# The far output product of dilated attention in four row-group parts: 32 keys at a time into four PSUM banks

## The chip, the cores and the metric

The kernel runs on one core of one Trainium2 chip. The metric is the device time of one execution in microseconds (us), from the median of several runs; the profile describes one such execution. The engines are TensorE (PE in the profile, with its weight loads shown apart as PEld), VectorE (DVE), ScalarE (ACT), GpSimd (POOL) and SyncE (SP), which only issues transfers here. TensorE multiplies a stationary operand of up to 128 rows (the contraction) by 128 columns, which a LDWEIGHTS puts into the array, with a moving operand that a MATMUL streams through it; the sums land in PSUM, which has eight banks of 512 float32 per partition.

## The reference

Two layers of a causal decoder trunk over 512 tokens of width 1024, in float32. Layer 0 mixes tokens with three groups of dilated sliding-window attention, eight heads of width 128 in each group; layer 1 with a pooling mixer; a SwiGLU FFN follows each. Only the attention of layer 0 touches this change:

```python
ATTN_PAIRS = ((128, 1), (512, 4), (2048, 16))
o = jnp.einsum('bnhqk,bnkhd->bnqhd', p / den, vb)   # per group, dilated by 1, 4, 16
wts = jax.nn.softmax(jnp.stack(lses, axis=0), axis=0)
o = jnp.sum(wts[..., None] * o, axis=0)             # the three groups of a head add up
return o.astype(h.dtype) @ w_out
```

With 512 tokens, group 0 (dilation 1) has four blocks of 128 queries that see their own and the previous block; group 1 (dilation 4) has four residue classes of 128 tokens, each a full 128 by 128 causal product; group 2 (dilation 16) has sixteen classes of 32 tokens, each a product of 32 queries with 32 keys. The kernel scales the probabilities of the three groups by the merge weights first, so that the outputs of a head are plain sums of three products.

## The kernel before

Everything is kept with channels on the 128 partitions and the 512 tokens along the free dimension. Projections are done in pairs by a scheme with seven half products instead of eight (`seven`, `values12`, and `chained` in the FFN); each weight is split in two fp32r parts by ACT (L92) and DVE (L93), and each product is three fp32r passes (L461 to L463, L632 to L634, L329 to L332). Weights stream from HBM through rings of buffers, in an order fixed by the queues `loads` and `steps`, which `pump` advances one step after each piece of a product.

Attention is written between those pieces. For heads 1 to 7 the loop runs `seven` for the query/key pair of each group, then the values; `between(h, g)` names the attention functions of an earlier head that are called after a given piece: for even h, `output(h-2)` after the second piece of g = 0 and `output(h-1)` after the third piece of g = 2. Heads 6 and 7 have their outputs after the loop, each followed by `halve`, which splits the result for the output projection (L1009 to L1018). The engines take their instructions in the order in which the functions are called; a wait is a semaphore that the program sets where one engine needs another's result or a free buffer.

Before `output(h)` come three steps on the same head. `scores0` and `scores12` form the scores (L716 for group 0 in pieces, L736 for group 1, L740 for group 2), `merge` scales the exponentials, and `turn0` and `turn12` transpose them, so that keys lie on the partitions: `own` and `before` hold group 0, `t12[:, 0]` group 1 and `t12[:, 1]` group 2. For group 2 four classes share the 128 partitions: class j takes partitions 32j to 32j+31, as a diagonal block of 32 by 32 in a 128 by 128 matrix that `zero` cleared once.

`output(h)` then multiplies values (stationary) with probabilities (moving), all in float32. The trace shows each float32 product of the program as two hardware passes, so that L847's 64 products stand there as 128 instructions.

- L840 and L841: seven products for group 0 into one PSUM bank, which ACT copies to `o[h]` in another order of the tokens (L843).
- L847: for each of four classes r the product of group 1 and that of group 2, which add up in a second bank. Group 2's product is a full 128 by 128 by 128 one, zeros included.
- L850: DVE adds the second bank to `o[h]`.

PSUM tiles come from one pool of eight banks (`ps`); a new tile takes a bank whose last reader is done.

Of the kernel before, what the change touches and what calls it, by code (L numbers as in the profile page):

```python
# [15 lines left out]
P = 128  # L16
S = 512
# [7 lines left out]
NT = S // P  # L25
NI = P // NT
G = P + NI
Y16 = NT * NT
# [12 lines left out]
WARM = 5  # L41
NOUT = 3
NSOLO = 2
PARTS = ((0, 2, False), (2, 10, True), (10, 18, True), (18, 22, False))
ENDS = 5
BACK = {"blocks": 3, "sums": 7}
# [19 lines left out]
def trunk(ctx: ExitStack, tc: tile.TileContext, xT, xN, norms, w_first, w_qk, w_qkp, w_v0, w_v0p, w_v12, w_out, w_outp, w_pair, w_down, w_dblock, w_pin, w_pgrp,  # L66
          consts, ident_in, invcnt_in, outT, outR):
    nc = tc.nc
# [14 lines left out]
    def ps():  # L83
        return psum.tile([P, S], F32, tag="ps", name="ps")
# [134 lines left out]
    def pairs(*srcs, shift=LINE // 4, back=False):  # L219

        these = [Pair(src, shift, back) for src in srcs]
        for parts in zip(*(p.steps() for p in these)):
            steps.extend(parts)
        units.append((these,))
# [11 lines left out]
    def plain(*srcs, lean=False):  # L236
        for src in srcs:
            share(1, src, lean=lean)

    for h in range(HEADS):  # L240
        if h == 0:
            plain(*[w_qk[u] for u in range(len(QK) - NF)])
        for g in range(3):
            if h == 1 and g < NSOLO:
                plain(*[w_qk[len(QK) - NF + 2 * g + c] for c in range(2)])
            elif h:
                pairs(w_qkp[3 * h - 3 - NSOLO + g])
        if h == 0:
# [10 lines left out]
    def ffn_plan(layer):  # L259
        j = 0  # L260
        for i, (first, end, block) in enumerate(PARTS):
            while j < min(max(end + block, NPLAIN), FC):
# [5 lines left out]
            if block:  # L268
                for m in range(K2):
                    pairs(w_dblock[sum(p[2] for p in PARTS) * layer + sum(p[2] for p in PARTS[:i]), m],  # L270
                          shift=0, back=True)
# [103 lines left out]
    def product(layer):  # L375
        return Product(KC, stream(layer)).add(range(KC)).p
# [27 lines left out]
    def rstd(parts):  # L404

        nt = parts[0].shape[1] // P
        pc = ps()
        for i, a in enumerate(parts):
            for t in range(nt):
                for c in range(0, P, NI):  # L410
                    nc.tensor.matmul(pc[c:c + NI, t:t + 1], a[:, t * P + c:t * P + c + NI], ones,
                                     start=i == t == 0, stop=i == len(parts) - 1 and t == nt - 1)
        v = tmp.tile([P, nt], F32, tag="var", name="var")
        nc.vector.tensor_scalar(v, pc[:, :nt], 1.0 / D, EPS, op0=OP.mult, op1=OP.add)
        r, n = tmp.tile([P, nt], F32, tag="rcol", name="rcol"), nt // 2
        for t in range(0, nt, n):
            nc.gpsimd.tensor_tensor(r[:, t:t + n], v[:, t:t + n], nhalf[:, :n], op=OP.pow)
        return [r[:, t:t + 1] for t in range(nt)]
# [177 lines left out]
    def in_a_row(t):  # L596
        return t.rearrange("p (y x z) -> p x y z", y=Y16, z=2)


    with tc.tile_pool(name="opool", bufs=1) as opool:  # L600
        early = [opool.tile([P, 2, S], F32R, tag=f"o{k}", name="early") for k in range(K2)]
        with tc.tile_pool(name="apool", bufs=1) as apool:
            const = apool.tile([P, 5 * P], F32, name="const")
            d0, d12, swap = const[:, :2 * G], (const[:, 2 * G:2 * G + P], const[:, 2 * G + P:3 * G]), const[:, 3 * G:3 * G + P]
            rows = {}
            QKV = {}
# [86 lines left out]
            def blk(t, b, n=1):  # L693
                return t[:, b * P:(b + n) * P]
# [136 lines left out]
            def output(h):  # L831
                (own, before), t12 = A[h]["t0"], A[h]["t12"]

                def v0(b):
                    return blk(QKV[h // 2, 0, 2][:, b, :], h % 2)

                po = ps()
                for b in range(NT):
                    if b > 0:
                        nc.tensor.matmul(blk(po, b), v0(b - 1), before[:, b - 1], start=True, stop=False)  # L840
                    nc.tensor.matmul(blk(po, b), v0(b), own[:, b], start=b == 0, stop=True)  # L841
                o0 = o[h]
                nc.scalar.copy(in_a_row(o0), po.rearrange("p (x y z) -> p x y z", y=Y16, z=2))  # L843
                po = ps()
                for r in range(NT):
                    for g in (1, 2):
                        nc.tensor.matmul(blk(po, r), blk(QKV[h // 2, 12, 2][:, r, :], h % 2 * 2 + g - 1),  # L847
                                         t12[:, g - 1, r, :],
                                         start=g == 1, stop=g == 2)
                nc.vector.tensor_add(o0, o0, po)  # L850


            late = [apool.tile([P, S], F32R, tag=tag, name="early") for tag in ("t0", "o0")]
# [5 lines left out]
            H, T, o = {}, {}, []  # L859
# [49 lines left out]
            for k in range(KC):  # L909
# [15 lines left out]
                for j, (w, v) in enumerate(((hi, 0), (hi, 1), (lo, 0))):  # L925
                    for i, f in enumerate(lead):
                        c = (k % 2 * NF + i) * P
# [34 lines left out]
            for c in range(2):  # L962
                p = product(0)
# [108 lines left out]
    with tc.tile_pool(name="fpool", bufs=2) as fpool:  # L1072
# [3 lines left out]
        def ftile(name, n=S):  # L1076
            return fpool.tile([P, PAD + S], F32, tag="f", name=name, bufs=6)[:, :n]
# [8 lines left out]
        def ffn(layer, nxt, lead, row):  # L1086
# [324 lines left out]
        r = rstd([t, sq])  # L1411
# [115 lines left out]
```

## Time and profile before

| | before |
|---|---|
| median of 3 runs | 1185.73 us (1185.5 to 1185.83) |
| span of the profiled execution, first to last instruction | 1184.0 us |
| PE busy | 1175.4 us (99%) |
| PEld busy (weight loads, overlapping PE) | 1119.9 us (95%) |
| DVE busy | 989.0 us (84%) |
| ACT busy | 721.7 us (61%) |
| POOL busy | 171.3 us (14%) |
| granted TensorE clock | 0.9 or more of full speed in every slice of the page |

For the profiled execution no time is given beside its span; the median of the runs lies 1.7 us above it. Attention with its projections runs from the start to about 435 us; the eight calls of `output` start at 112, 139, 214, 241, 316, 343, 420 and 430 us.

How to read the rows: a group row gives line, engine, operation, what it writes and reads, rows and columns of the stationary operand (128*32), size of the moving one (128x32), the count, then busy time in us (overlaps counted once), the mean ns of one, the engine's idle time before them and what ended it. A MATMUL's duration includes its way through the array, so consecutive ones overlap; the pace is the distance from start to start. A chain row gives start, length and the work on the path that ended last. A timeline row gives start, length and, in brackets, the engine's idle time before it.

### The profile page before, as it was taken

How to read it: one execution, taken by the hardware profiler on the slowest of the kernel's cores; microseconds unless marked ns; L12 is line 12 of the kernel's file. 1: busy time of each engine (PE TensorE's matmuls, PEld its weight loads, DVE VectorE, ACT ScalarE, POOL GpSimd, SP SyncE). 2: the span in 40 equal slices, each digit the busy share in tenths (PEclk: the TensorE clock that was granted, in tenths of full speed). 3: DMA queues.
4: the chain of work that ended last, by engine and by line, in shares of the span. 5: the costliest groups of instructions: out<-in, count | busy, mean ns of one | idle time of the engine just before them, and what ended most of it. 6: DMA issues, size and time to landing. Idle time of an engine off the chain costs nothing.

```text
span 1184.0 us, 25180 instructions
## 1 busy us (share of the span) xinstructions
PE 1175.4 (99%) x10042; PEld 1119.9 (95%) x10042; DVE 989.0 (84%) x1733; ACT 721.7 (61%) x1262; POOL 171.3 (14%) x165
## 2 busy tenths in 40 slices
PE   9999999999999999999999999999999999999997
PEld 7889999999999989889999999988889999999997
DVE  7997898889789888699988988656789998898875
ACT  6554564546455557747756775775575766676553
POOL 1101111111111002311111111122130111111100
PEclk9999999999999999999999999999999999999999
DMA  8537667666856557957777877798595777877732
GB/s 302 130 95 187 147 153 166 168 160 152 192 140 169 145 157 195 246 113 203 191 188 189 204 184 209 195 265 208 121 195 119 187 199 195 198 191 193 197 92 72
DMA packets 83766, 207.57 MB, mean 175 GB/s; under 512 B 7856, under 2 KB 13120, under 8 KB 83648
## 3 DMA queue, kind: packets, MB, share of 16 engines
q1 hardware_dynamic: 52672, 144.84, 36.9%
q0 software_dynamic: 30688, 60.83, 31.6%
q8 instruction: 78, 1.28, 0.4%
q14 instruction: 40, 0.33, 0.1%
q10 hardware_dynamic: 288, 0.29, 0.1%
HBM read 203.84 MB, written 2.10 MB: 174 GB/s over the span
## 4 chain that ended last, share of the span: by engine, by line
PE 96%; DMA 1%; issue 1%; DVE 1%; ACT 0%; POOL 0%; POOLq 0%; DVEq 0%; ACTq 0%
PE ps L461 21%; PE ps L462 20%; PE ps L463 20%; PE ps L329 7%; PE ps L330 7%; PE ps L332 7%; PE ps L928 2%; PE ps L632 2%; PE ps L633 2%; PE ps L634 2%; DMA raw<-w_outp 1%; PE ps L847 1%; PE ps L716 1%; PE ps L736 1%; PE ps L841 1%
## 5 line engine op out<-in xcount | busy, mean ns | idle before, releaser
L92 ACT ACTIVATE w<-raw 128x1024 fp32r<-128x1024 f32 x268 | 283.7, 1063 | 177.0 <-PE ps L463 73.3
L93 DVE TENSOR_TENSOR w<-raw,w 128x1024 fp32r<-128x1024 f32 x268 | 326.4, 1222 | 48.8 <-ACT w L92 44.7
L461 PE MATMUL ps<-far,w 128*128 128x256 f32 x896 | 246.5, 275 | 0.0
L462 PE MATMUL ps<-far,w 128*128 128x256 f32 x896 | 246.4, 275 | 0.0
L463 PE MATMUL ps<-far,w 128*128 128x256 f32 x896 | 246.4, 275 | 0.0
L461 PE MATMUL ps<-near,w 128*128 128x256 f32 x676 | 190.5, 282 | 0.0
L462 PE MATMUL ps<-near,w 128*128 128x256 f32 x676 | 186.9, 277 | 0.0
L463 PE MATMUL ps<-near,w 128*128 128x256 f32 x676 | 186.9, 276 | 0.0
L462 PEld LDWEIGHTS ps<-far,w 128*128 128x128 f32 x896 | 168.2, 188 | 0.1
L461 PEld LDWEIGHTS ps<-far,w 128*128 128x128 f32 x896 | 168.2, 188 | 0.1
L463 PEld LDWEIGHTS ps<-far,w 128*128 128x128 f32 x896 | 168.2, 188 | 0.0
L461 PEld LDWEIGHTS ps<-near,w 128*128 128x128 f32 x676 | 127.1, 188 | 0.5
L462 PEld LDWEIGHTS ps<-near,w 128*128 128x128 f32 x676 | 127.1, 188 | 0.0
L463 PEld LDWEIGHTS ps<-near,w 128*128 128x128 f32 x676 | 127.0, 188 | 0.0
L329 PE MATMUL ps<-near,w 128*128 128x512 f32 (+1 forms) x316 | 119.4, 379 | 0.0
L332 PE MATMUL ps<-near,w 128*128 128x512 f32 (+1 forms) x316 | 118.7, 376 | 0.0
L330 PE MATMUL ps<-near,w 128*128 128x512 f32 (+1 forms) x316 | 118.7, 376 | 0.0
L173 POOL DMA_DIRECT2D raw<-w_pair x36 | 43.6, 1210 | 291.7 <-DMA raw<-w_pair 87.3
L329 PEld LDWEIGHTS ps<-near,w 128*128 128x128 f32 x316 | 59.3, 188 | 11.0 <-ACT near L92 0.4
L332 PEld LDWEIGHTS ps<-near,w 128*128 128x128 f32 x316 | 59.3, 188 | 10.9
L330 PEld LDWEIGHTS ps<-near,w 128*128 128x128 f32 x316 | 59.4, 188 | 10.6 <-DVE near L93 0.2
L92 ACT ACTIVATE half<-rawhalf 128x512 fp32r<-128x512 f32 x84 | 52.8, 630 | 13.7 <-PE ps L463 11.8
(333 smaller groups left out, 2802.7 us busy)
## 6 DMA issues: line engine op xcount, KB each, us to landing
raw<-w_pair SPq DMA_DIRECT2D x80, 512.0 KB, 4.9
raw<-w_qkp SPq DMA_DIRECT2D x38, 512.0 KB, 4.5
raw<-w_pair POOLq DMA_DIRECT2D x36, 512.0 KB, 7.6
raw<-w_dblock SPq DMA_DIRECT2D x32, 512.0 KB, 4.7
raw<-w_qkp POOLq DMA_DIRECT2D x19, 512.0 KB, 7.5
raw<-w_v SPq DMA_DIRECT2D x18, 512.0 KB, 4.1
rawhalf<-w_pair SPq DMA_DIRECT2D x36, 256.0 KB, 5.2
raw<-w_dblock POOLq DMA_DIRECT2D x16, 512.0 KB, 7.5
```

The costliest lines, as they stand in the source:

```text
L92: nc.scalar.activation(hi, v, AF.Copy)
L93: nc.vector.tensor_tensor(lo, v, hi.bitcast(F32), op=OP.subtract)
L173: nc.gpsimd.dma_start(self.b.rearrange("p (a c) -> p a c", a=2), self.src[:, None, 3 * n:].to_broadcast([P, 2, n]), accum_op=OP.add)
L329: nc.tensor.matmul(self.p[:, cols], w[0][:, s], mh[:, cols], start=self.done == 0, stop=False)
L330: nc.tensor.matmul(self.p[:, cols], w[0][:, s], ml[:, cols], start=False, stop=False)
L332: nc.tensor.matmul(self.p[:, cols], w[1][:, s], mh[:, cols], start=False, stop=self.done == self.n)
L461: nc.tensor.matmul(dst, w.t[0][:, c], th, start=k == 0 and not on, stop=False, skip_group_check=on)
L462: nc.tensor.matmul(dst, w.t[0][:, c], tl, start=False, stop=False, skip_group_check=on)
L463: nc.tensor.matmul(dst, w.t[1][:, c], th, start=False, stop=k == n - 1, skip_group_check=on)
L632: nc.tensor.matmul(o, mh, wh, start=k == 0, stop=False)
L633: nc.tensor.matmul(o, mh, wl, start=False, stop=False)
L634: nc.tensor.matmul(o, ml, wh, start=False, stop=k == K2 - 1)
```

## The change

Only `output` is changed. Group 0's seven products now write straight into the place of their tokens in the final order: the destination is a view of the bank in runs of two neighbouring columns, 32 columns apart. Group 1's four products add to the same bank. Group 2's products are cut along the keys: for each class r four products of 32 keys (rows 32c to 32c+31 of the array), 128 channels and 32 queries, part c into a bank of its own, in 32 columns of it. ACT then copies the shared bank to `o[h]`, and DVE adds the four others, each to a quarter of `o[h]`'s columns. The zeros outside the diagonal blocks are no longer multiplied.

```diff
+ROWS = 4
...
                 po = ps()
+                rows = in_a_row(po)
+
+                def put(dst, v, w, first=False):
+                    nc.tensor.matmul(dst, v, w, start=first, stop=True, skip_group_check=True)
...
                 for b in range(NT):
+                    dst = rows[:, b * NT:(b + 1) * NT]
+                    put(dst, v0(b), own[:, b].rearrange("p (x y z) -> p x y z", y=Y16, z=2), b == 0)
                     if b > 0:
-                        nc.tensor.matmul(blk(po, b), v0(b - 1), before[:, b - 1], start=True, stop=False)
-                    nc.tensor.matmul(blk(po, b), v0(b), own[:, b], start=b == 0, stop=True)
-                o0 = o[h]
-                nc.scalar.copy(in_a_row(o0), po.rearrange("p (x y z) -> p x y z", y=Y16, z=2))
-                po = ps()
+                        put(dst, v0(b - 1), before[:, b - 1].rearrange("p (x y z) -> p x y z", y=Y16, z=2))
                 for r in range(NT):
-                    for g in (1, 2):
-                        nc.tensor.matmul(blk(po, r), blk(QKV[h // 2, 12, 2][:, r, :], h % 2 * 2 + g - 1),
-                                         t12[:, g - 1, r, :],
-                                         start=g == 1, stop=g == 2)
-                nc.vector.tensor_add(o0, o0, po)
+                    put(blk(po, r), v12(r, 1), t12[:, 0, r, :])
+                far = [ps()[:, :S // ROWS].rearrange("p (r q) -> p r q", r=NT) for c in range(ROWS)]
+                n = P // ROWS
+                for r in range(NT):
+                    for c in range(ROWS):
+                        k = slice(c * n, (c + 1) * n)
+                        put(far[c][:, r], v12(r, 2)[k], t12[k, 1, r, k], r == 0)
+                nc.scalar.copy(o[h], po)
+                for c in range(ROWS):
+                    oc = o[h].rearrange("p (r c q) -> p c r q", r=NT, c=ROWS)[:, c]
+                    nc.vector.tensor_add(oc, oc, far[c])
```

`v12(r, g)` is the block of values of class r for group g, as L847 read it.

On PE the stretch of `output(0)`, called from `between(2, 0)`, stands in the program before as follows. L461 to L463 are the projection around it; `t0` holds group 0's probabilities, `t12` the others', `v0` and `v12` the values.

```order
L463 MATMUL ps_1288<-h_658,w_1188 128x256
L841 MATMUL ps_1331<-t0_845,v0_615 128x128
L840 MATMUL ps_1331<-t0_845,v0_615 128x128
L841 MATMUL ps_1331<-t0_845,v0_615 128x128
L840 MATMUL ps_1331<-t0_845,v0_615 128x128
L841 MATMUL ps_1331<-t0_845,v0_615 128x128
L840 MATMUL ps_1331<-t0_845,v0_615 128x128
L841 MATMUL ps_1331<-t0_845,v0_615 128x128
L847 MATMUL ps_1340<-t12_905,v12_1028 128x128 x8
L461 MATMUL ps_1289<-near_82,w_1204 128x256
```

In the changed program the same stretch reads (its lines lie one or more further down; only the first of four rounds of parts is shown, and the other three are the same):

```order
L842 MATMUL ps_1331<-t0_845,v0_615 128x4x16x2 x7
L842 MATMUL ps_1331<-t12_905,v12_1028 128x128 x4
L842 MATMUL ps_1343<-t12_905,v12_1028 128x32
L842 MATMUL ps_1344<-t12_905,v12_1028 128x32
L842 MATMUL ps_1345<-t12_905,v12_1028 128x32
L842 MATMUL ps_1346<-t12_905,v12_1028 128x32
```

Four full products of L847 became sixteen of 32 keys and 32 columns, which go round four banks (ps_1343 to ps_1346), after all full ones; the number of products goes from 15 to 27 per head.

On DVE the end of the same `output` stands so before (L93 and L190 prepare weights, L771 and L774 belong to `merge`):

```order
L93 TENSOR_TENSOR w_1402<-raw_1181,w_1402 128x1024
L850 TENSOR_TENSOR o_1024<-o_1024,ps_1340 128x512
L771 TENSOR_TENSOR far_1229<-ps_1369,place_453 128x64
L774 TENSOR_REDUCE st_935<-far_1229 128x16
```

and so in the changed program:

```order
L94 TENSOR_TENSOR w_1420<-raw_1181,w_1420 128x1024
L863 TENSOR_TENSOR o_1024<-o_1024,ps_1343 128x4x32
L863 TENSOR_TENSOR o_1024<-o_1024,ps_1344 128x4x32
L863 TENSOR_TENSOR o_1024<-o_1024,ps_1345 128x4x32
L863 TENSOR_TENSOR o_1024<-o_1024,ps_1346 128x4x32
L772 TENSOR_TENSOR far_1229<-ps_1387,place_453 128x64
```

One add of 512 columns became four of 128, at the same place in DVE's queue; ACT's copy stays at its place too.

More of the change, by code (lines that the diff above doesn't have):

```diff
@@ L837, in output, with v12 @@
                 po = ps()
+                rows = in_a_row(po)
+                def put(dst, v, w, first=False):
+                    nc.tensor.matmul(dst, v, w, start=first, stop=True, skip_group_check=True)
+                def v12(r, g):
+                    return blk(QKV[h // 2, 12, 2][:, r, :], h % 2 * 2 + g - 1)
                 for b in range(NT):
+                    dst = rows[:, b * NT:(b + 1) * NT]
+                    put(dst, v0(b), own[:, b].rearrange("p (x y z) -> p x y z", y=Y16, z=2), b == 0)
                     if b > 0:
-                        nc.tensor.matmul(blk(po, b), v0(b - 1), before[:, b - 1], start=True, stop=False)
-                    nc.tensor.matmul(blk(po, b), v0(b), own[:, b], start=b == 0, stop=True)
-                o0 = o[h]
-                nc.scalar.copy(in_a_row(o0), po.rearrange("p (x y z) -> p x y z", y=Y16, z=2))
-                po = ps()
-                for r in range(NT):
-                    for g in (1, 2):
-                        nc.tensor.matmul(blk(po, r), blk(QKV[h // 2, 12, 2][:, r, :], h % 2 * 2 + g - 1),
-                                         t12[:, g - 1, r, :],
-                                         start=g == 1, stop=g == 2)
-                nc.vector.tensor_add(o0, o0, po)
+                        put(dst, v0(b - 1), before[:, b - 1].rearrange("p (x y z) -> p x y z", y=Y16, z=2))
+                for r in range(NT):
+                    put(blk(po, r), v12(r, 1), t12[:, 0, r, :])
[9 more added lines that the diff above has]
+                    nc.vector.tensor_add(oc, oc, far[c])
             late = [apool.tile([P, S], F32R, tag=tag, name="early") for tag in ("t0", "o0")]
```

## The prediction

> **What bounds the kernel now.** I read the page first (busy times, chain shares), then the waits, then the chain and the timeline around the eight calls of `output`.
>
> ```profile
> span 1184.0 us, 25180 instructions
> PE 1175.4 (99%) x10042; PEld 1119.9 (95%) x10042; DVE 989.0 (84%) x1733; ACT 721.7 (61%) x1262; POOL 171.3 (14%) x165
> PE 96%; DMA 1%; issue 1%; DVE 1%; ACT 0%; POOL 0%; POOLq 0%; DVEq 0%; ACTq 0%
> ```
>
> TensorE carries 96% of the path and is never idle for long, so whatever `output` adds to or takes from PE's queue moves the end by as much. Busy share does not say whether streaming or weight loading paces PE. The chain shows what one output costs there (start, length, work):
>
> ```profile
> 140.35 1.79 PE ps L847 x16
> 142.14 0.12 PE ps L461
> ...
> 153.04 0.89 PE ps L736 x8
> 153.93 0.39 PE ps L740 x32
> 154.32 0.31 PE ps L461
> 154.63 0.12 PE ps L462
> ```
>
> L847's sixteen passes take 1.79 us, 0.112 each; eight of them are group 2's, so 0.89 us per head is what the change replaces, 7.2 us over eight heads: the most that could ever be saved. Group 0 and group 1 keep their passes. The lower four rows are the nearest thing to the new form: L740 works on a 32-column strip of the array (128*32), four strips side by side.
>
> **What a small tile costs.** Two things are read from L740 and its kin: the pace inside, and what going in and out costs.
>
> ```profile
> 153.86 0.35 PEld L740 LDWEIGHTS ps<-qk,qk 128*32 128x32 f32 x32
> 477.71 0.35 PEld L411 LDWEIGHTS ps<-ones,sq 128*32 128x32 f32 x32 [0.35 <-issue]
> 161.31 0.31 PEld L769 LDWEIGHTS ps<-far,const 128*128 128x128 f32 x2
> L847 PEld LDWEIGHTS ps<-t,v 128*128 128x128 f32 x128 | 14.9, 192 | 0.0
> L740 PEld LDWEIGHTS ps<-qk,qk 128*32 128x32 f32 x256 | 2.8, 112 | 1.0
> L740 PE MATMUL ps<-qk,qk 128*32 128x32 f32 x256 | 3.7, 199 | 0.0
> L411 PE MATMUL ps<-ones,sq 128*32 128x1 f32 x160 | 2.3, 172 | 0.0
> ```
>
> In L740, 32 loads start within 0.35 less one load's 0.112, that is 0.24 us or about 0.0077 each: four strips take a round of four in 0.031 us. L411 streams one column where L740 streams 32, yet its 32 loads take the same 0.35 us. So in these tiles the loads set the pace and not the streaming. A load of 128 columns lasts 192 ns and one of 32 lasts 112: 80 ns for 96 columns, 0.83 ns a column, so 128 columns occupy 0.107 us, all but L847's pace of 0.112. L769 confirms it for the full array: it streams only 64 columns, but its two loads stand 0.31 less 0.19, 0.12 us apart.
>
> The change shortens what is streamed (128 columns to 32) and the contraction (128 rows to 32). It leaves every weight tile 128 columns wide, which is the dimension that a load's time follows in these rows; none of them has fewer than 128 rows. Instead of 8 loads per head there are 32.
>
> The Trainium skill says outright what no run here can show: by TensorE: Matmul & The Clock Gate, section LDWEIGHTS, a load's time goes with its columns alone, and one of 32 rows by 128 columns takes as long as a full one. Its figure for 128 columns, an estimate of 107 ns at 1.2 columns per ns, is what the rows above give (0.107 us). By it the row groups can at best hide the extra loads, not gain; the sum below would be the same.
>
> Going in and out: 32 passes of L740 are eight rounds, 8 x 0.031 = 0.25 us, but take 0.39 in the chain, so 0.14 us is lost on the way in; the next full pass (L461) takes 0.31 instead of 0.12, so 0.19 on the way out. Together 0.33 us each time that the array changes its tiling. `output` has no such change now and gets one per head.
>
> **The sum.** Per head 16 products of 32 keys are 32 passes, four row groups with 8 each.
>
> - If the four row groups run side by side as L740's four strips do, a row group loads 8 x 0.112 = 0.89 us, as long as the 0.89 us removed. The net is the change of tiling, +0.33 us.
> - Bound above: the groups' loads go one after another, 32 x 0.112 = 3.58 us, net 3.58 + 0.33 - 0.89 = +3.02 us per head.
> - Bound below: a load costs by its area and 32x128 passes go at the round of a 128x32 tile, 0.031 us: 0.25 + 0.33 - 0.89 = -0.31 us per head.
>
> I take the first: L740 is nearest in every respect (four tiles, float32, 32 columns streamed), and a round there overlaps four tiles' loads.
>
> Group 0's seven products write the same columns in runs of two; no row has a strided destination. Below, it costs nothing; above, I let each of the 14 passes take twice its 0.112, +1.57 us per head. I take zero: a float32 pass at 0.112 for 128 columns has 0.87 ns for each column to land. The Trainium skill has a rule against it: PSUM — Partial Sum Buffer, section Specifications (TRN2), warns that a non-contiguous pattern slows matmuls significantly, and gives PSUM lines of 8 bytes. The runs here are just 8 bytes long and no run shows such a write; the rule gives no factor, and it is the rival below.
>
> Off PE:
>
> ```profile
> L850 DVE TENSOR_TENSOR o<-o,ps 128x512 f32<-128x512 f32 x8 | 5.5, 685 | 6.1 <-PE ps L847 6.1
> L508 DVE TENSOR_TENSOR sums<-ps,qk 128x256 f32<-128x256 f32 x12 | 4.5, 411 | 0.1
> L843 ACT COPY o<-ps 128x512 f32<-128x512 f32 x8 | 4.9, 607 | 4.3 <-PE ps L841 4.3
> 342.41 0.41 DVE L516 TENSOR_TENSOR qk<-sums,ps 128x256 f32<-128x256 f32 x1
> ```
>
> 256 columns less are 274 ns less, so an add of 128 columns should take 685 - 3 x 137 = 274 ns, four 1.10 us: +0.41 us of DVE per head, 3.3 in all. DVE waits 6.1 us for L847 at its eight adds, so it is early at nearly all of them and this is hidden. Were it not, it would be at most 0.4 us a head. ACT's copy has the same size, but now waits for group 1 as well, some 0.9 us longer, with the next weights' splits queued behind it; PE has no wait for those now (the waits below), and ACT is busy 61%.
>
> Five banks instead of two are taken per output. A far bank may be had when its last reader is through. For odd heads the last reader ahead is L516 of the pair before; the one above ended at 342.82 and `output(5)` reaches L847 at 344.63, so 1.8 us are spare, and the far products start 0.9 us later still. No wait there, and at most some tenths if DVE slips.
>
> The one place where PE waits for other engines lies between the last two outputs:
>
> ```profile
> PE ps L841 <- ACT t L808: 0.8, 1, 0.8
> 408.77 10.49 DMA raw<-w_outp
> 426.53 0.68 DVE L850 TENSOR_TENSOR o<-o,ps 128x512 f32<-128x512 f32 x1
> 427.73 0.62 ACT L92 ACTIVATE near<-o 128x512 fp32r<-128x512 f32 x1
> 429.57 0.49 PE L841 MATMUL ps<-t,v 128*128 128x128 f32 x2 [0.81 <-ACT t L808]
> ```
>
> `output(7)` starts 0.81 us late, behind a chain of transfer, DVE and ACT that begins before `output(6)` at 420. What output 6 adds on PE is swallowed there, so seven heads count, not eight. The first six count in full: the transfer waits for buffers that PE's progress frees, so it moves with them. DVE's extra 0.41 us at 426.53 ends L850 at 427.62 instead of 427.21, just ahead of the ACT split at 427.73 that needs it; uncovered it would cost up to 0.4 us once.
>
> Sum: 7 x 0.33 = +2.3 us. The profiled span of 1184.0 becomes 1186.3; with the 1.7 us that lie between span and median, **1188.0 us**.
>
> **The rivals.**
>
> - Row groups share more than L740's strips do. Two at a time make 16 rounds: 1.79 + 0.33 - 0.89 = +1.23 us per head, less the 0.8 swallowed once: +9.0, 1194.8 us. One at a time: 8 x 3.02 - 0.8 = +23.4, 1209.1 us. For it: no row shows two row groups at once. Against it: strips overlap freely. Chance 16%.
> - The strided destination halves group 0's pace: 8 x 1.57 + 2.3 = +14.9, less what is left of the swallowed 0.8, 0.5: 1200.1 us. For it: nothing in these rows excludes it. Against: 8 bytes in one piece. Chance 12%.
> - The other side, a gain: loads of 32 rows are cheaper than those of 128. At the round of 0.031 us each of seven heads gains 0.31 us, 1183.6 us, and it decides from a round below 0.070 us (8 x 0.070 + 0.33 = 0.89). For it: no row has a load with fewer rows. Against: 0.83 ns a column in each load seen. TensorEngine Tiling (Array Packing) of the Trainium skill, section Theoretical Speedup, promises up to four times for a contraction of 32; its Key Properties name the drain at a change of mode, with which L740's 0.33 us agrees. Taken at full value, and without the drain, 0.89 becomes 0.22 and seven heads gain 4.7 us: 1181.0 us. Chance together 8%.
> - The rest, 2%, is waits for PSUM banks of a few us.
>
> **How the numbers follow.** The forecast has 62%. Its own range is 1186.7 (entry or exit cheaper by half) to 1189.5 (0.2 us more per head). Two tenths of a per cent, about what a measurement of this kernel tells from no change, are 2.4 us; the forecast of +2.3 lies at that line. Of its 62 points I give 29 to slower and 33 to the same. The two rivals above it are slower, 28; of the gain's 8 points I give 5 to faster and 3 to the same, since its 1183.6 is just within the line, and the rest falls 1 to slower, 1 to faster. That makes faster 6%, same 36%, slower 58%. The range 1185.0 to 1200.5 holds the forecast, two groups at a time and the strided case, and leaves out the gain (8%) and one group at a time (8%).
>
> **What would show it.** In the changed profile the 32-row loads of one output should span about 0.9 us with rounds of four some 0.112 us apart; rounds of 0.031 mean the gain, loads each 0.112 after the last mean the serial rival. The full pass after them should take about 0.3 us in the chain instead of 0.12. Group 0's 14 passes should keep 0.112 us each. The four DVE adds should take about 0.27 us each, and the wait list should name only L841's counterpart on ACT, longer or shorter by some tenths. The prediction is wrong if PE waits for DVE or ACT at the far products, or if seven outputs lengthen by other than 0.33 us each.

## The result and the profile after

| | before | changed |
|---|---|---|
| median of 18 runs each, on the same chips | 1186.2 us (1185.29 to 1187.23) | 1188.04 us (1187.74 to 1188.93) |
| span of the profiled execution | 1184.0 us | 1186.8 us |
| DVE busy | 989.0 us | 990.6 us |
| PE instructions | 10042 | 10234 |

The changed kernel takes 1.0016 times as long, with a 95% interval of 1.0010 to 1.0022: 1.2 to 2.6 us slower. Page of the changed kernel, its first rows and the shares of the chain by engine:

```profile
span 1186.8 us, 25595 instructions
PE 1179.2 (99%) x10234; PEld 1122.4 (95%) x10234; DVE 990.6 (83%) x1757; ACT 721.4 (61%) x1262; POOL 170.5 (14%) x165
PE 99%; issue 1%; DVE 0%; POOL 0%; DVEq 0%; POOLq 0%
```

The path now is PE alone. Before, DVE and DMA had 1% each of it; the reason is the short stretch between the last two outputs, told below. The chain around the second output (start, length, work; the change moves line numbers, so that L842 holds all of `output`'s products, and L461 became L462):

```profile
139.81 3.48 PE ps L842 x54
143.29 0.32 PE ps L462
143.61 0.13 PE ps L463
```

and the timeline of its weight loads, and then the groups of L842, of the four adds and of ACT's copy:

```profile
142.20 0.98 PEld L842 LDWEIGHTS ps<-t,v 32*128 32x128 f32 x32
```

```profile
L842 PEld LDWEIGHTS ps<-t,v 128*128 128x128 f32 x176 | 20.4, 192 | 0.5 <-ACT t L809 0.5
L842 PEld LDWEIGHTS ps<-t,v 32*128 32x128 f32 x256 | 7.9, 186 | 1.0
L863 DVE TENSOR_TENSOR o<-o,ps 128x128 f32<-128x128 f32 x32 | 7.0, 282 | 6.9 <-PE ps L842 6.7
L860 ACT COPY o<-ps 128x512 f32<-128x512 f32 x8 | 4.7, 581 | 8.0 <-PE ps L842 8.0
```

The 32 loads of one head start within 0.98 less one load's 0.19, that is 0.79 us. In single records a round is four loads 6.7 ns apart, and the rounds start 0.108 to 0.112 us after one another (142.197, 142.305, 142.414, 142.526 us and so on). So the four row groups do run side by side, but a load of 32 rows lasts 186 ns where one of 128 rows lasts 192, and each round takes as long as one full pass. The Trainium skill's page TensorE: Matmul & The Clock Gate has this rule in its section LDWEIGHTS (a load's time goes with its columns); the two rows above agree with it.

From the start of the last full pass to the start of the second full pass behind, one head takes 1.450 us, where before its eight full passes of the third group and the next one took 1.125: +0.325. Group 0's 14 passes, now with a strided destination, still stand 0.112 us apart. The changed kernel's only wait of PE for another engine:

```profile
PE ps L921 <- DVE idle L918: 1.2, 1, 1.2
```

It was there before, at L908, in the first 5 us of the program; the prediction had called the last output the one place where PE waits. PE waits for no PSUM bank and for nothing at the far products. The wait of 0.8 us of the last output for ACT is gone, while the prediction expected it to be the only one on the list.

Where the time came from is seen by matching PE's passes outside `output` one by one (there are 9802 in both traces). The difference of their start times, changed less before, in us:

| output | last pass ahead of it | second pass behind it | step over the output | step up to the next output |
|---|---|---|---|---|
| 0 | +0.73 | +1.05 | +0.32 | -0.03 |
| 1 | +1.02 | +1.35 | +0.33 | +0.18 |
| 2 | +1.53 | +1.85 | +0.32 | -0.03 |
| 3 | +1.82 | +2.15 | +0.33 | +0.18 |
| 4 | +2.33 | +2.65 | +0.32 | -0.03 |
| 5 | +2.62 | +2.95 | +0.33 | +0.18 |
| 6 | +3.13 | +3.41 | +0.28 | 0.00 |
| 7 | +3.41 | +2.74 | -0.67 | +0.09 to the end |

The first 0.73 arises in the first 15 us, before any changed instruction, and stays constant up to the first output. In the other kernels below it lies anywhere from -0.02 to +0.74, so it belongs to the execution and not to the edit. Without it the profile says +2.1 us, the medians +1.84: seven outputs +2.23, the stretches between them +0.45, the last output -0.67, the end +0.09.

**The stretches between.** Timeline of PE behind output 1, before and then changed; each fence shows the first and the last of a run of equal passes:

```profile
142.33 0.28 PE L461 MATMUL ps<-near,w 128*128 128x256 f32 x1
...
143.58 0.28 PE L463 MATMUL ps<-near,w 128*128 128x256 f32 x1
```

```profile
144.04 0.28 PE L462 MATMUL ps<-tx,w 128*128 128x256 f32 x1
...
145.10 0.28 PE L462 MATMUL ps<-near,w 128*128 128x256 f32 x1
```

Before, 11 passes lie between these two, 1.25 / 11 = 0.114 us each; changed, 9 passes, 1.06 / 9 = 0.118. Over the whole stretch of 96 passes the means are 113.4 and 117.8 ns, at a granted clock of 1.00 in both: 96 x 4.4 ns = 0.42 us. Before had such a slower stretch too, the 60 passes behind the scores (L740) that follow: 117.8 ns there before, 113.6 in the changed kernel, which gives back 0.24 us. So +0.18 after every odd output.

**The last output.** Chain of the kernel before, ahead of its last output, then the timeline of the changed one at the same place:

```profile
424.91 0.32 DVE t L809
...
425.25 0.43 DVE room L1029
...
426.19 0.43 DVE room L1030
...
426.71 0.63 ACT oh L92
427.34 0.12 ACT t L806
```

```profile
427.18 1.24 DVE L810 STREAM_TRANSPOSE t<-s 32x128 f32<-32x128 f32 x4
...
429.45 0.21 ACT L807 COPY t<-ps 32x96 f32<-32x96 f32 x1
...
432.12 0.42 DVE L1043 TENSOR_TENSOR room<-room,o 128x256 f32<-128x256 f32 x1
...
433.16 0.63 ACT L93 ACTIVATE oh<-room 128x512 fp32r<-128x512 f32 x1
```

Before, DVE's second half of `room` (L1030) and ACT's split of it stand between the last transposes and the copies of `turn0` that the last output waits for. The transposes end at 425.23, and the first copy starts at 427.25 on ACT's timeline: 2.0 us. In the changed program the same two instructions (L1043 and the split at 433.16) stand behind those copies, and the way from 428.42 to 429.45 takes 1.0 us. PE came to this place 3.41 us later than before, the last copy that its first product needs ended only 2.64 us later (432.16 against 429.52), and of the 0.81 us of waiting 0.04 are left. Up to the transposes the chain had kept step with PE (3.2 us later); it got ahead behind them. Some of that was lost again, since ACT now waits for the four adds there:

```profile
430.36 0.63 ACT L93 ACTIVATE near<-o 128x512 fp32r<-128x512 f32 x1 [0.33 <-DVE o L863]
```

Another part of the -0.67 is the order of group 0's products. Weight loads before, then PE in the changed kernel:

```profile
430.07 0.30 PEld L840 LDWEIGHTS ps<-t,v 128*128 128x128 f32 x2 [0.20 <-ACT t L806]
```

```profile
432.21 1.54 PE L842 MATMUL ps<-t,v 128*128 128x128 f32 x11
```

Before, the second product (L840, with `before`) waits for the last copy of `turn0` on ACT, which ends at 430.02 us. In the changed kernel a product with `own` stands ahead of it, and PE runs on; by the single records this saves 0.22 us. So the last output adds up: +0.33 for its own change of tiling, -0.77 of waiting, -0.22 by the order of the products.

### The profile page after: what moved, and what is told of

Read it like the earlier page. It is cut to its first block, busy times and chain, and to the rows that moved or that the text cites. A ratio compares the mean times of both kernels' runs of the same rounds, so it can differ in the third digit from the quotient of the medians.

```text
span 1186.8 us, 25595 instructions
## 1 busy us (share of the span) xinstructions
PE 1179.2 (99%) x10234; PEld 1122.4 (95%) x10234; DVE 990.6 (83%) x1757; ACT 721.4 (61%) x1262; POOL 170.5 (14%) x165
## 4 chain that ended last, share of the span: by engine, by line
PE 99%; issue 1%; DVE 0%; POOL 0%; DVEq 0%; POOLq 0%
PE ps L462 21%; PE ps L463 20%; PE ps L464 20%; PE ps L330 8%; PE ps L333 8%; PE ps L331 8%; PE ps L842 2%; PE ps L633 2%; PE ps L635 2%; PE ps L634 2%; PE ps L941 2%; PE ps L717 1%; PE ps L737 1%; PE ps L921 0%; PE ps L425 0%
## 5 line engine op out<-in xcount | busy, mean ns | idle before, releaser
L93 ACT ACTIVATE w<-raw 128x1024 fp32r<-128x1024 f32 x268 | 283.6, 1063 | 176.9 <-PE ps L464 72.9
L462 PE MATMUL ps<-far,w 128*128 128x256 f32 x896 | 246.5, 275 | 0.0
L463 PE MATMUL ps<-far,w 128*128 128x256 f32 x896 | 246.5, 275 | 0.0
L462 PE MATMUL ps<-near,w 128*128 128x256 f32 x676 | 190.8, 282 | 0.0
L463 PE MATMUL ps<-near,w 128*128 128x256 f32 x676 | 187.0, 277 | 0.0
L462 PEld LDWEIGHTS ps<-far,w 128*128 128x128 f32 x896 | 168.2, 188 | 0.1
L463 PEld LDWEIGHTS ps<-far,w 128*128 128x128 f32 x896 | 168.2, 188 | 0.1
L462 PEld LDWEIGHTS ps<-near,w 128*128 128x128 f32 x676 | 127.1, 188 | 0.7
L463 PEld LDWEIGHTS ps<-near,w 128*128 128x128 f32 x676 | 127.1, 188 | 0.0
L93 ACT ACTIVATE half<-rawhalf 128x512 fp32r<-128x512 f32 x84 | 52.8, 630 | 13.9 <-PE ps L464 11.8
```

What stands on the lines that cost most here:

```text
L93: nc.scalar.activation(hi, v, AF.Copy)
L462: nc.tensor.matmul(dst, w.t[0][:, c], th, start=k == 0 and not on, stop=False, skip_group_check=on)
L463: nc.tensor.matmul(dst, w.t[0][:, c], tl, start=False, stop=False, skip_group_check=on)
```

## The experiments

The theory: a round of row groups takes what a load of its columns takes (0.112 us for 128), and changing the tiling costs about 0.33 us per head. Rivals: it is the strided or shared bank, the extra DVE adds, or work off PE that costs the 1.8 us. Each diff is against the changed kernel. Medians are of 4 to 11 runs, and each ratio is against the kernel before on the same chip (medians 1186.51, 1186.07 and 1186.3 us in the three sets). "Section" is the time from the last full pass ahead of the far products to the second full pass behind them; it is 1.125 us before and 1.450 in the changed kernel.

### rows_alone: the parts on row groups, the rest as before

```diff
-                    dst = rows[:, b * NT:(b + 1) * NT]
-                    put(dst, v0(b), own[:, b].rearrange(...), b == 0)
...
+                    nc.tensor.matmul(blk(po, b), v0(b), own[:, b], start=b == 0, stop=True)
+                o0 = o[h]
+                nc.scalar.copy(in_a_row(o0), po.rearrange("p (x y z) -> p x y z", y=Y16, z=2))
+                po = ps()
...
+                nc.vector.tensor_add(o0, o0, po)
```

> The row-group half of the change alone: group 0 into a bank of its own with contiguous columns and the permuting ACT copy, as before, group 1 into a second bank, group 2 in four row parts into four banks; DVE adds five times. Theory (the loss is the change of tiling on TensorE, 0.33 us per head): the same loss as the changed kernel, 1187.5 to 1188.8 us beside 1186.2 before, and each row-group section about 0.9 us plus 0.33. Rival (the loss comes from the strided destination and the shared bank): 1186.2, no change. DVE gets about 0.7 us more per head; if that mattered, 1190 and PE waits would show.

Measured: 1189.35 us, ratio 1.0031 (1.0019 to 1.0044). The section is that of the changed kernel, 1.450 us, and the offsets step by the same +0.33 over the first six outputs. So the row parts alone account for the change's loss. The time is 0.5 us above the expected range, and the list of PE's waits shows why:

```profile
PE ps L330 <- DVE o L861: 1.4, 1, 1.4
```

Behind output 6 the next product waits for DVE's add that reads the second bank. With a sixth bank and a fifth add per output it most likely waits for a bank to be given back: the rows name the releaser and not the reason. The prediction's margin of banks thus does not hold for every number and order of banks (far_first, below, waits at the same place with five).

### one_bank: groups 0 and 1 in one strided bank, the third group as full products

```diff
-                far = [ps()[:, :S // ROWS].rearrange("p (r q) -> p r q", r=NT) for c in range(ROWS)]
...
+                full = ps()
                 for r in range(NT):
-                    for c in range(ROWS):
...
+                    put(blk(full, r), v12(r, 2), t12[:, 1, r, :], r == 0)
                 nc.scalar.copy(o[h], po)
+                nc.vector.tensor_add(o[h], o[h], full)
```

> The other half alone: groups 0 and 1 add up in one bank with the strided destination, group 2 stays a full 128-row product into a second bank, one DVE add. Theory: TensorE has the same 30 passes at 0.112 us and no change of tiling, so 1186.2 as before, within 0.7 us; the 14 passes of group 0 at 0.112 us. Rival: the strided destination or the later ACT copy cost something, then 1188.

Measured: 1186.21 us, ratio 0.9999 (0.9990 to 1.0007). The offset against before is the same ahead of and behind each of the first seven outputs (+0.56), so neither the strided destination nor the shared bank costs anything.

### all_in_one: all fifteen full products in one bank, no DVE add

```diff
                 for r in range(NT):
-                    put(blk(po, r), v12(r, 1), t12[:, 0, r, :])
-                far = ...
...
+                    for g in (1, 2):
+                        put(blk(po, r), v12(r, g), t12[:, g - 1, r, :])
                 nc.scalar.copy(o[h], po)
-                for c in range(ROWS):
-                    oc = o[h].rearrange("p (r c q) -> p c r q", r=NT, c=ROWS)[:, c]
-                    nc.vector.tensor_add(oc, oc, far[c])
```

> All 15 products of a head add up in one bank, in full 128-row form, one ACT copy, no DVE add. Theory: TensorE's passes are those of before, so 1186.2; if the 0.8 us for which TensorE waits before the last output goes with the shorter DVE queue, 1185.4. If DVE's adds had been on the path, 5.5 us less DVE would show as more than 1 us.

Measured: 1185.82 us, ratio 0.9996 (0.9987 to 1.0005). DVE is busy 984.0 us, 5.0 less than before, and it moves nothing: the adds were hidden. The waits of PE for ACT ahead of the last output, of one_bank and then of all_in_one:

```profile
PE ps L842 <- ACT t L809: 0.7, 1, 0.7
```

```profile
PE ps L842 <- ACT t L809: 1.1, 1, 1.1
```

In one_bank the split of `room` stands ahead of the copies on ACT, as it did before. In all_in_one it stands behind them, as in the changed kernel, and PE still waits. But the rest of the order is not that of the changed kernel: DVE's second half of `room` stays ahead, and ACT's copy of `o` (427.50 us) has moved in between. In the kernels below and in rows_alone, PE doesn't wait for the copies where the split stands behind them (rows_alone, halves, by_group, far_first); where it stands ahead, PE waits 0.2 to 1.0 us (cols64, quarters, far_twice; not in cols32). In far_twice it waits although it comes there 9.1 us later than before, so lateness alone doesn't do it either. The order goes with the wait; what else it takes stays open. The 0.22 us from the order of group 0's products is in both kernels: the last output steps by -0.28 in one_bank, whose wait is 0.06 us shorter than before, and by +0.08 in all_in_one, whose wait is 0.30 longer.

### no_far: without the third group's products and adds

```diff
-                far = ...
-                for r in range(NT):
-                    for c in range(ROWS):
...
-                for c in range(ROWS):
-                    oc = ...
-                    nc.vector.tensor_add(oc, oc, far[c])
```

> The changed kernel without group 2's product (no far products, no adds): it leaves out the whole third group. It measures what the section is worth. Theory (everything in it is on the path of TensorE): 8 x (0.89 + 0.33) = 9.8 us less than the changed kernel's 1188.0, 1178.3, or up to 0.8 more where a wait before the last output returns: 1178 to 1179.5. Rival (the section is partly hidden behind waits): above 1181.

Measured: 1178.47 us, ratio 0.9931 (0.9918 to 0.9943): 9.6 us under the changed kernel. Eight rounds of 0.112 and 0.33 of tiling change for eight heads are 9.8 us. What the parts cost is on PE, and nothing else of size hangs on them.

### halves: two row groups of 64

```diff
-ROWS = 4
+ROWS = 2
```

> Two row groups of 64 keys instead of four of 32: 8 products, 16 passes, two at a time, 64 columns streamed, two banks, two DVE adds of 256 columns. Theory (a round is paced by loading 128 columns, whatever the rows and the columns streamed): eight rounds of 0.112 us again, so the same 1188.0, within 0.7. Rival (the time follows the area, or the contraction): rounds other than 0.112 us; at 0.056 a round 1184.4.

Measured: 1187.9 us, ratio 1.0014 (1.0004 to 1.0023). Timeline of one head's loads, and the chain around them:

```profile
142.03 0.97 PEld L842 LDWEIGHTS ps<-t,v 64*128 64x128 f32 x16
```

```profile
139.65 3.49 PE ps L842 x38
143.14 0.32 PE ps L462
```

Sixteen loads take as long as thirty-two did (0.97 against 0.98 us), and the section is 1.465 us. The number of row groups, of products and of adds plays no part: it is eight rounds either way. The stretches between the outputs keep their pace here (113.4 ns behind output 1), and the offset steps by 0.34 over each of the first six outputs and by 0.00 between.

### by_group: the same products, one row group after the other

```diff
-                for r in range(NT):
-                    for c in range(ROWS):
+                for c in range(ROWS):
+                    for r in range(NT):
```

> The changed kernel with the order of the sixteen part products turned round: all four classes of row group 0, then of row group 1, and so on. Same products, same banks. Theory with strictly ordered passes: each group's eight passes follow one another at 0.112 us, 32 x 0.112 = 3.58 instead of 0.89 us per head, 1188.0 + 8 x 2.7 = 1209.5 us. Rival (the array takes loads for other row groups ahead out of a deep queue, so that order does not matter): 1188.0.

Measured: 1207.21 us, ratio 1.0178 (1.0163 to 1.0193). This lies near the 1209.5 us of strictly serial groups, but the trace has another mechanism. Timeline of one head's loads, then the windows of PE around two outputs (window; its us, PE's busy us and passes; granted clock, DMA share, GB/s), then the timeline of PE behind output 1:

```profile
143.26 2.38 PEld L842 LDWEIGHTS ps<-t,v 32*128 32x128 f32 x32
```

```profile
120.00:143.00 23.00, 23.00 (x279) 1.00 0.60 135
143.00:147.00 4.00, 4.00 (x42) 0.89 0.86 187
147.00:160.00 13.00, 13.00 (x133) 0.90 0.44 103
...
222.00:226.00 4.00, 4.00 (x42) 0.83 0.90 290
```

```profile
146.38 0.42 PE L463 MATMUL ps<-near,w 128*128 128x256 f32 x1
146.59 0.42 PE L464 MATMUL ps<-near,w 128*128 128x256 f32 x1
```

The 32 loads start within 2.2 us (2.38 less 0.19), not 3.58. The records don't name the row group, but the spacing tells: in output 0 the first five loads stand 0.11 us apart, and the sixth follows 0.03 us behind the fifth (115.470 against 115.437 us). So the first load of the next group starts there, and the last three of its own group overlap it. That is +1.40 us per head. The rest is the clock. The windows above are means; inside them the clock stands at 0.50 for 3.4 us, from 146.1 us on:

```profile
146.20:149.40 3.20, 3.20 (x18) 0.50 0.88 127
```

The same comes from 224.6, 255.4, 333.9 and 364.6 us on, once at each of outputs 1 to 5, and not at outputs 0 and 6. Ordinary passes then stand 0.21 us apart instead of 0.11. The offset against before grows by 1.3 to 1.7 us in each of the stretches from output 1 to output 6, 7.8 us in all, where the changed kernel has 0.5. Of the 17.9 us between the profiled executions of by_group and of the changed kernel the outputs thus make about 11 and the stretches about 7. In the changed kernel the same windows have a clock of 1.00. That the time came near the forecast of serial groups is luck. The interleaved order is what makes four row groups cost no more than full products.

### cols64 and cols32: also cut in columns

cols64 cuts each part in two halves of 64 columns, cols32 in four of 32:

```diff
-                        put(far[c][:, r], v12(r, 2)[k], t12[k, 1, r, k], r == 0)
+                        for m in range(0, P, 64):
+                            put(far[c][m:m + 64, r], v12(r, 2)[k, m:m + 64], t12[k, 1, r, k], r == 0)
```

> The part products cut also along the channels: tiles of 32 rows by 64 columns, 32 products, 64 passes, eight tiles side by side, each load 64 columns. Theory (loads pace the rounds at 0.83 ns a column): rounds of about 0.058 to 0.062 us, 8 x 0.06 + 0.33 = 0.81 us per head against 0.89 before and 1.22 in the change: 1184.7 us. Rival (a round costs 0.112 however wide the tile, or issue limits it): 1188 or more.

> Tiles of 32 rows by 32 columns: 64 products, 128 passes, sixteen tiles side by side. Loads alone would allow rounds of 0.031 us, 1183; but a round has 32 instructions, and in the column-strip code four tiles (8 instructions) go in 0.031 us, 0.0039 each, so I expect issue to bind: 0.125 us a round, 8 x 0.125 + 0.33 = 1.33 us per head, 1188.9. It tells the two limits apart.

Measured: cols64 1186.94 us, ratio 1.0008 (0.9999 to 1.0018); cols32 1195.25 us, ratio 1.0076 (1.0061 to 1.0091). Timeline of one head's loads in cols64, and then in cols32:

```profile
141.22 0.75 PEld L842 LDWEIGHTS ps<-t,v 32*64 32x64 f32 x64
```

```profile
142.08 1.18 PEld L842 LDWEIGHTS ps<-t,v 32*32 32x32 f32 x128
```

Fewer columns do shorten the loads: by the groups of L842 one lasts 130 ns with 64 columns and 103 with 32, against 186 with 128. Single records of cols64 tell more. The rounds of eight tiles start 0.055, 0.056, 0.059 and 0.058 us after one another, as the columns let expect, then 0.173 and twice 0.067, in every head alike. So after 33 loads comes a pause of 0.11 us, and from there a load every 0.067 / 8 = 0.0084 us. In cols32 the rounds of sixteen go the same way: one or two of 0.061 to 0.067 us, a pause, and then 0.133 us each, 0.0083 a load. It is a pace per instruction, no longer one per column. The section is 1.215 us in cols64, 0.24 less than in the changed kernel and still 0.09 more than before; in cols32 it is 1.642. Both lie above what was expected (1184.7 and 1188.9 us). In cols64 that is the pause and the pace behind it, 0.17 us a head, and a slower stretch after each odd output (+0.23). PE's waits in cols32 show a second price:

```profile
PE ps L463 <- issue: 3.0, 1, 3.0
PE ps L331 <- issue: 1.2, 1, 1.2
```

PE is idle for 3 us behind the third output, waiting for nothing that the profile shows. The clock then stands at 0.50 for 3.4 us:

```profile
224.10:227.40 3.30, 3.30 (x17) 0.50 0.99 153
```

Together the two cost 4.7 us by the offset, and the stretch with the second idle time 1.35. As to the cause, the queue that carries instructions has 86 packets instead of 80 in the changed kernel. That PE's instructions came late is likely, but no run here shows it apart.

### quarters: 64 by 64 tiles

ROWS = 2 and the column cut of cols64 together: four tiles, 32 loads per head.

> Tiles of 64 rows by 64 columns: 16 products, 32 passes, four tiles side by side, two banks, two DVE adds. The tiles of 32 by 64 took 0.0098 us a load and 0.078 a round of eight, those of 32 by 32 took 0.0084 a load, so few loads of few columns are wanted. Theory (a round is the longer of loading, 64 x 0.83 ns = 0.053, and issue, 4 x 0.0084 = 0.034): rounds of 0.058 us, from the last full pass to the second full pass after it about 1.03 us against 1.13 before, 1.45 in the changed kernel and 1.22 with 32 by 64: 1185.4 us, or 1186.2 if the wait before the last output returns. Rival (a section's switching costs more when rows and columns are both cut): no faster than the 1186.9 of 32 by 64.

Measured: 1186.02 us, ratio 1.0000 (0.9991 to 1.0009). Loads on the timeline, the chain around the section, and the wait ahead of the last output:

```profile
141.23 0.56 PEld L842 LDWEIGHTS ps<-t,v 64*64 64x64 f32 x32
```

```profile
138.85 3.08 PE ps L842 x54
141.93 0.32 PE ps L462
```

```profile
PE ps L842 <- ACT t L809: 1.0, 1, 1.0
```

A round starts 0.055 to 0.059 us after the one before, half of 0.112, without a pause at 32 loads, and the section is 1.051 us, 0.074 less than before. This is the only form whose section beats full products. But the last output waits again, 1.0 us, and part of the gain goes to a slower pace between an odd output and the next (48 passes at 165 us run at 117.8 ns; the offset grows by 0.23 in that stretch). Over seven heads the gain is 0.5 us at most, below what can be measured here.

### far_twice: the far products twice

```diff
+                for i in range(2):
                     for r in range(NT):
                         for c in range(ROWS):
...
+                            put(far[c][:, r], v12(r, 2)[k], t12[k, 1, r, k], i == r == 0)
```

> The changed kernel with group 2's sixteen products done twice into the same banks, so the third group counts double in the output: two sets of eight rounds, one change of tiling. Theory (a fixed 0.33 us and 0.112 us a round): 8 x 0.89 = 7.2 us above the changed kernel, 1195.2 us. Rival (the fixed part is the drain of each bank or of each set): more than that by 8 x 0.1 or so. If a longer stretch at a quarter of the array's work lowers the granted clock, as it did with the order by groups, more than 1196.

Measured: 1195.37 us, ratio 1.0078 (1.0064 to 1.0092). Chain:

```profile
140.18 4.37 PE ps L842 x86
144.55 0.32 PE ps L462
```

The section is 2.343 us. Eight more rounds cost 0.893 us, 0.112 each, with no second cost of the tiling change; 8 x 0.893 = 7.1 us, and 7.3 were measured. The rounds and the fixed 0.33 us are thus told apart. The granted clock stays at 1.00 around the outputs, although the far products now last 1.7 us.

### far_first: the far products ahead of the other groups'

Only their place in `output` is changed: the loop over r and c stands ahead of group 0's products.

> The changed kernel with the row-group products ahead of the products of groups 0 and 1 instead of behind them; the same passes and the same change of tiling. It asks about the pace of the projection passes after an output: in the changed kernel 96 of them run at 117.8 ns after the odd heads' outputs instead of 113.4 before, +0.42 us three times, partly given back later. If what the array did last sets that pace, full float32 passes now stand before the projection as in the kernel before: 113.4 ns there, and 1187.3 us. If the pace follows from something else, 1188.0 and no change.

Measured: 1189.16 us, ratio 1.0024 (1.0014 to 1.0033), slower than expected. The pace answers as expected. The stretch behind output 1 is back at 113.4 ns, with full products between the parts and the projections:

```profile
143.56 0.28 PE L463 MATMUL ps<-near,w 128*128 128x256 f32 x1
...
144.69 0.28 PE L464 MATMUL ps<-near,w 128*128 128x256 f32 x1
```

Between these two lie 10 passes, 1.13 / 10 = 0.113 us each. The step behind output 1 is 0.00 instead of +0.18. That the last work on the array sets the pace isn't shown by this: in halves, quarters and cols64 parts stand last too, and the same stretch runs at 113.4 ns. Behind the same scores (L740) the pace is 117.8 ns before and 113.6 in the changed kernel. The step over an output is +0.33 here as well, wherever in `output` the parts stand. But a new wait of PE takes more than the pace gave; the wait, and ACT's timeline ahead of it:

```profile
PE ps L330 <- ACT o L860: 1.4, 1, 1.4
```

```profile
428.41 0.57 ACT L860 COPY o<-ps 128x512 f32<-128x512 f32 x1
```

In the changed kernel this copy behind output 6 starts at 426.33 us, ahead of a split of `room`; here it stands behind that split. It is again the order of the other engines near the last two outputs that PE meets.

## Why the prediction was right, and where it was not

- **Loads pace the parts.** Right. Eight rounds at 0.112 us and loads of 186 ns at 32 rows are what the forecast took from L740 and L847; far_twice gives the round directly, halves shows that the number of row groups doesn't matter.
- **The tiling change, 0.33 us per head.** Right: +0.32 to +0.33 at the first six outputs, +0.28 at the seventh, where the passes around it stream 512 columns.
- **The rivals.** Two groups or one at a time: fallen in the interleaved order (rounds of four 0.11 us apart). The strided destination: fallen, by one_bank and by group 0's unchanged 0.112 us. The Trainium skill's rule in PSUM — Partial Sum Buffer, section Specifications (TRN2), didn't bind here. A gain from small row counts: fallen; the best form here, quarters, halves the round instead. The speedup of up to four times that the Trainium skill gives in TensorEngine Tiling (Array Packing), section Theoretical Speedup, isn't seen in row groups of 128 columns.
- **DVE and ACT.** Right in the main: all_in_one, with no add at all, is no faster by a measurable amount. One add takes 282 ns where 274 was forecast, but four that overlap take 0.87 us and not 1.10, so DVE is busy 1.6 us longer in all and not 3.3. The one case that the forecast left open came: behind output 6 ACT waits 0.33 us for the adds. No wait of PE followed. ACT waits 8.0 us for L842 instead of 4.3, and nothing follows from it.
- **Banks.** Right, no wait; but rows_alone, with one bank more, and far_first, with five in another order, each wait 1.4 us behind output 6, a place for which the forecast had worked out no margin.
- **Seven heads count, output 6 being swallowed.** This step failed. The forecast let the chain ahead of the last output stay as it was, with 0.33 us of its 0.81 us wait swallowed, so that output 6 and the last output together would add 0.33 us. They add +0.28 and -0.67. Nearly the whole wait went (-0.77), at a place where the built order of DVE and ACT changed: the split of `room` moved out from ahead of the copies. And `own` standing ahead of `before` saved 0.22 us that no term of the sum had. The order of both programs could be compared beforehand. That the place of the split alone removes the wait isn't shown (all_in_one), and what else it takes stays open.
- **Every other pass keeps its pace.** Assumed without being said, and wrong: +0.18 us behind each odd output, 0.45 in all after the small gains behind even ones. Before already had both paces (113.4 behind L847, 117.8 behind L740), so the rows to suspect it were there. What sets the pace stays open.
- **The sum.** Forecast +2.3, the profile +2.1, the medians +1.84. The two missed terms, +0.45 and -0.67, nearly cancel, and that is luck: it is why 1188.0 met 1188.04 so closely. The median of three runs it started from was 0.5 us below that of the 18; the closeness owes something to that too. The lower end of the range, 1186.7, is said to be entry or exit cheaper by half; half of 0.19 us over seven heads is 0.7 us and gives 1187.3, so that end was wider than its reason.

## What to carry to other kernels

Cutting a product into row groups removes multiplications by zero and no time as long as each weight tile keeps its columns: count rounds times the load of one tile's columns, and add the price of entering and leaving the tiling (0.33 us here) for each stretch. Only cutting columns too shortened a round, and of these forms 64 by 64 tiles with 32 loads in one go were best; even they were not measurably faster than full products. Interleave the groups. When an edit shifts a scheduled program, compare the built order at each place where the engine that sets the end waits today, not only at the edit.

## What the runs showed of the hardware beyond that

- Identical full passes of 256 columns run at 113.4 or 117.8 ns for a whole stretch, at a granted clock of 1.00. Behind output 1 it is the slower pace in the changed kernel, rows_alone and far_twice (four interleaved row groups of 128 columns last), and the faster one in one_bank and far_first (full products last) but also in halves and quarters, where row groups come last too. Where that stretch is slow, the one behind the next scores is fast (113.6 ns), and the other way round (117.8). What sets the pace stays open.
- Row groups used one after another (by_group) halved the granted clock for 3.4 us at five of the eight outputs, after 2.2 us of such loads, while twice as many interleaved rounds over 1.7 us (far_twice) left it at 1.00. Whether the quarter of the array in use or the length decides was not tried. In cols32 the same drop followed an idle time of PE of 3.0 us.
- PE looked ahead over few loads: in by_group the next row group starts behind the fifth of eight loads, by the spacing of the records, so order decides how much overlaps.
- The smallest tiles go fast only for a while: the first 16 to 32 loads of a section come 4 ns apart (cols32), and after a pause it is 8.3 ns each, in every head. And cols32, with 768 more matmuls than the changed kernel, twice left PE without work, for 3.0 and 1.2 us.
